# Float16 halves of the cached keys and values: made tile by tile in the attention units and kept in DRAM, instead of in the last stage

## Chip, cores and metric

One core of one Trainium2 chip. The metric is the device time of one launch in microseconds, the median of several runs; lower is better. A profiled execution is one more run, with the hardware profiler on.

## The reference, cut to what matters

One layer of a streaming encoder, for 2048 new frames of one prompt and for 16 new frames of each of 8 running streams that bring a cache of 512 positions. Two attention branches run beside each other on the same normalised input:

```python
# d = 1024; branch a: 4 heads of (2 x 64 keys, 128 values); branch b: 8 heads of 64
h = rms_norm(x) * (1 + scale) + shift
qa, ka, va, za, qb, kb, vb, zb, ga, gb = split(h @ w_in)         # qa, ka rotated by position
# a: two softmaxes over the keys, o = (p1 - lam * p2) @ va, mask by chunks of 64
# b: stick-breaking: a = sigmoid(z) * exp(sum of log_sigmoid(-z) over later keys), o = a @ vb, causal
ya = (rms_norm(oa) * 0.8 * silu(za)) @ w_branch_a
yb = (ob * silu(zb)) @ w_branch_b
y  = rms_norm(x + gate * ((sigmoid(ga) * ya + sigmoid(gb) * yb) @ w_out))
# the sample streams: the same, with keys = concat(cache_a_k, ka), values = concat(cache_a_v, va), and so for b
```

All inputs and outputs are float32. The four caches (`cache_a_k`, `cache_a_v`, `cache_b_k`, `cache_b_v`) are 8 x 512 positions x 512 numbers each, 8.4 MB. The outputs are the two results and the new keys and values.

## The kernel before

**Halves.** TensorE works on float16. To keep the accuracy of float32, an operand x is scaled by a power of two s and split into `hi` = float16(s x) and `lo` = float16(s x - hi), and a product takes three matmuls, hi*hi, hi*lo and lo*hi. `split` (line 294) makes the halves: `hi` on ACT, POOL or DVE, `lo` always on DVE with one `scalar_tensor_tensor`. The scale comes from a bound, the sum of squares of the whole operand: `sum_squares` (line 274) squares on ACT and adds along a row, `total` (line 215) adds over the 128 partitions with a matmul against a matrix of ones, and `scales` (line 221) cuts the exponent out of it with a few DVE steps on 1 to 16 columns, which gives s and 1/s.

**Stages.** A first stage computes the modulation and hT, the halves of the transposed normalised input, which stay in DRAM (`hT_d`). Then come eight *units* u = 0..7, one head of branch a (even u) or two heads of branch b (odd u) each. In a unit, tile t = NT is the sample's 128 rows and t = 0..15 are the prompt's. Three streams of work are interleaved on the engines: the projections (L435, with gates in L511), about five tiles ahead of the rest (`LEAD`), which load hT tile by tile into one of three `hs` buffers (`fetch_h`, L412); the scores of tile t (L646, L647), with the softmax (L565, L610) or the stick-breaking product (L623 scans on DVE, L629 on POOL); and the product of weights and values two tiles later (`PV_LAG`; L703 to L708), for which the weights' halves are transposed by a transfer within SBUF (`turn`, L587, into `wt`). Three PSUM banks "s" serve the scores. While unit u runs, `prepare_unit(u + 1)` loads and splits the next unit's weights into buffers of 4 KB per partition out of the list `free`; its pieces stand in `back`, a few of them per tile from the unit's first tile on.

**Squares of the caches.** The scale of a cached head needs the sum of squares of all of it. `norms` (line 845) makes a list `spare` of 80 pieces, each a load of 128 x 1024 numbers into a buffer of `free` and one square on ACT: 16 pieces of the branch and output weights and 64 of the caches (4 caches x 4 heads x 4 pieces). A tile with an empty `back` takes some of `spare` (lines 1264 to 1269), so they go where no unit is being prepared. The caches are loaded here for the squares alone and dropped.

**Last stage.** After the units, 17 tiles pass through the branch and output products (`branches` L1322, `turned`, `turned_y` L1172, `output` L1351); for each tile, `inputs` loads o, z and g from DRAM (L1180 to L1185), ACT makes sigmoids and halves. Beside the first 13 of them (`S_TILES`) runs the attention of the samples over the caches, `sample` (line 729), in a lane of steps, six of them later for each unit (`S_PERIOD`). Here each cached piece is loaded once more as float32 into one of three `dc` buffers (L755, L757). Keys are split with `hi` on ACT into `k16c` and then transposed within SBUF into `dks` (L764); values are split into `v16c` and used as they are. Scores of the samples are L782, outputs L810.

**Queues.** All transfers named here are issued by SP, in program order; an instruction that waits holds back what stands behind it. The order on every engine is made by the framework's scheduler from the order of the calls.

Of the kernel before, what the change touches and what calls it, by code (L numbers as in the profile page):

```python
# [16 lines left out]
F32 = mybir.dt.float32  # L17
# [32 lines left out]
S_PERIOD = 6  # L50
H_AT = 2
# [61 lines left out]
def layer_kernel(ctx: ExitStack, tc: tile.TileContext, a: dict):  # L113
# [6 lines left out]
    def act(**kw):  # L120
# [20 lines left out]
    values_by_block = {  # L141
        "av": a["cache_a_v"][0].rearrange("b (j p) h e -> p j b (h e)", p=P),
        "bv": a["cache_b_v"][0].rearrange("b (j p) h d -> p j b (h d)", p=P),
    }
# [29 lines left out]
    gate_d = dram.tile([9, D], F32, name="gate_d")  # L174

# [39 lines left out]
    def total(col, n=1):  # L215

        p = bank("t")
        T.matmul(p[:, 0:n], ones, col, start=True, stop=True)
        return p[:, 0:n]
# [62 lines left out]
    def add_up(acc, n):  # L282
# [4 lines left out]
        return col  # L287

    def add_up_all(acc):
        col = tiny.tile([P, acc.shape[1]], F32, tag="cols", name="cols", bufs=1)  # L290
        V.tensor_reduce(out=col, in_=acc, axis=AX.X, op=ALU.add)
        return col
# [107 lines left out]
    csums = con.tile([P, 16, 4], F32, name="csums")  # L400
# [328 lines left out]
    def sample(U, dec, qpad, cs, parity):  # L729
# [6 lines left out]
        sk, ik, sv, iv = (cs[:, i : i + 1] for n in (nk, nv) for i in (cache_column(n, h), 16 + cache_column(n, h)))  # L736
# [15 lines left out]
        def cache(name, i):  # L752
            box[name, i] = kc = dec.tile([P, 8, P], F32, tag="dc", name="dc", bufs=3)
            if name == nv:
                load(out=kc, in_=values_by_block[name][:, i, :, h * P : (h + 1) * P])  # L755
            else:
                load(out=kc, in_=caches[name][:, i * 8 : i * 8 + 8, h * P : (h + 1) * P])  # L757

        def keys(i):
            kc = box.pop((nk, i))  # L760
            k16 = dec.tile([P, 16, 2, 64], F16, tag="k16c", name="k16c", bufs=2)
            split(k16[:, :, 0, :], k16[:, :, 1, :], kc.rearrange("p j (c d) -> p (j c) d", c=2), sk, S)
            box["k", i] = kt = dec.tile([P, 8, 2, P], F16, tag="dks", name="dks", bufs=4)
            nc.sync.dma_start_transpose(out=kt.rearrange("p j c n -> p (j c) n"), in_=k16.rearrange("p j f d -> p (j f d)"))  # L764
# [671 lines left out]
```

## Time and profile before

| | |
|---|---|
| median of 3 runs | 2340.79 us (2339.63 to 2344.61) |
| the profiled execution | 2345.66 us |
| its span, first to last instruction | 2343.9 us |
| busy share of the span: PE, DVE, ACT, POOL | 90%, 73%, 71%, 28% |
| mean granted TensorE clock | 0.965 |
| moved by DMA | 445.29 MB in 834,498 packets, mean 190 GB/s |
| HBM read, written | 245.60 MB, 69.24 MB |

In the profile PE is TensorE (its weight loads apart as PEld), DVE VectorE, ACT ScalarE, POOL GpSimd and SP the engine that issues transfers. `L302` is line 302 of the kernel before. A row of a group has the instruction, what it writes and reads, its shape and count, and times; "idle before" and waits say how long an engine stood and what ended the wait. Matmuls overlap in the pipeline, so the mean time of one is longer than its share of PE.

### The profile page before, as it was taken

How to read it: one execution, taken by the hardware profiler on the slowest of the kernel's cores; microseconds unless marked ns; L12 is line 12 of the kernel's file. 1: busy time of each engine (PE TensorE's matmuls, PEld its weight loads, DVE VectorE, ACT ScalarE, POOL GpSimd, SP SyncE). 2: the span in 40 equal slices, each digit the busy share in tenths (PEclk: the TensorE clock that was granted, in tenths of full speed). 3: DMA queues.
4: the chain of work that ended last, by engine and by line, in shares of the span. 5: the costliest groups of instructions: out<-in, count | busy, mean ns of one | idle time of the engine just before them, and what ended most of it. 6: DMA issues, size and time to landing. Idle time of an engine off the chain costs nothing. (4 is left out here: it accounts for less than half of the span.)

```text
span 2343.9 us, 41533 instructions
## 1 busy us (share of the span) xinstructions
PE 2104.1 (90%) x14688; PEld 1119.9 (48%) x14688; DVE 1714.2 (73%) x3661; ACT 1656.7 (71%) x3260; POOL 664.1 (28%) x578
## 2 busy tenths in 40 slices
PE   5998898988989899899999989999996869788998
PEld 3654454545545445445545544554553434334443
DVE  4658765779865677978667797877778868777663
ACT  4968777788877788778677777866777656665641
POOL 1222022356400334630034473103345121111111
PEclk7999999999999999999999999999997989999999
DMA  9777659797785997877587877756687999998421
GB/s 335 274 213 177 154 117 275 175 201 166 208 204 126 219 203 190 174 184 188 134 194 174 189 171 180 195 145 145 148 177 167 284 253 242 240 241 239 147 102 48
DMA packets 834498, 445.29 MB, mean 190 GB/s; under 512 B 537354, under 2 KB 777274, under 8 KB 833776
## 3 DMA queue, kind: packets, MB, share of 16 engines
q1 hardware_dynamic: 833340, 442.24, 75.7%
q8 instruction: 115, 1.88, 0.3%
q14 instruction: 95, 0.78, 0.1%
q10 hardware_dynamic: 948, 0.39, 0.1%
HBM read 245.60 MB, written 69.24 MB: 134 GB/s over the span
## 5 line engine op out<-in xcount | busy, mean ns | idle before, releaser
L629 POOL TENSOR_TENSOR sc_p<-sc_p,sc_n 128x127 f32<-128x127 f32 (+7 forms) x192 | 313.4, 1637 | 826.7 <-DVE sc_n L623 813.0
L435 PE MATMUL ps_mm<-wb,hs 128*128 128x512 f16 x1632 | 415.9, 383 | 0.1
L435 PEld LDWEIGHTS <-hs 128*128 128x128 f16 x3120 | 274.8, 99 | 256.6 <-DMA hs<-hT_d 10.9
L435 PE MATMUL ps_mm<-wa,hs 128*128 128x512 f16 x1488 | 374.5, 382 | 10.6 <-DVE qbuf L470 6.7
L623 DVE TENSOR_TENSOR_SCAN sc_n<-ps_s,sc_n,zero_t 128x512 f32<-128x512 f32 x192 | 245.4, 1278 | 68.2 <-ACT ps_s L122 64.7
L646 PE MATMUL ps_s<-k,qst 128*128 128x512 f16 (+3 forms) x640 | 225.3, 353 | 32.7 <-DVE sc_n L623 24.1
L580 DVE TENSOR_TENSOR sc_n<-sc_p,sc_n 128x128 f16<-128x128 f32 (+7 forms) x192 | 212.6, 1111 | 57.1 <-ACT sc_n L579 56.7
L511 PEld LDWEIGHTS <-hs 128*128 128x128 f16 x1632 | 156.5, 98 | 188.0 <-ACT qst L539 6.1
L122 ACT ACTIVATE sc_p<-ps_s,usc 128x512 f32<-128x512 f32 (+3 forms) x320 | 204.7, 640 | 32.7 <-PE ps_s L647 25.2
L647 PE MATMUL ps_s<-k,qst 128*128 128x512 f16 (+3 forms) x640 | 225.9, 354 | 0.0
L579 ACT CAST sc_n<-sc_p 128x128 f16<-128x128 f32 (+7 forms) x192 | 155.4, 813 | 77.5 <-POOL sc_p L629 77.2
L707 PE MATMUL ps_o<-v,wt 128*128 128x128 f16 x1088 | 172.7, 226 | 36.9 <-DMA wt<-sc_n 36.8
L511 PE MATMUL ps_t<-wa,hs 128*128 128x512 f16 x816 | 193.2, 383 | 7.6 <-ACT qst L539 6.0
L122 ACT ACTIVATE ps_s<-ps_s,usc 128x512 f32<-128x512 f32 (+3 forms) x328 | 199.8, 609 | 0.0
L511 PE MATMUL ps_t<-wb,hs 128*128 128x512 f16 x816 | 191.5, 379 | 1.1 <-DVE fsq L343 0.6
L1351 PE MATMUL ps_o<-wo,wb 128*128 128x512 f16 x816 | 186.1, 382 | 5.6 <-ACT wb L1173 5.6
L708 PE MATMUL ps_o<-v,wt 128*128 128x64 f16 x1088 | 159.1, 199 | 0.0
L707 PEld LDWEIGHTS <-wt 128*128 128x128 f16 x1088 | 105.8, 102 | 104.5 <-DMA wt<-sc_n 50.5
L565 DVE TENSOR_SCALAR_CACHE_REDUCE sc_p<-ps_s,usc 128x512 f32<-128x512 f32 (+3 forms) x160 | 106.3, 665 | 44.5 <-PE ps_s L647 30.7
L623 DVE TENSOR_TENSOR_SCAN sc_n<-ps_s,zero_t 128x128 f32<-128x128 f32 (+3 forms) x128 | 104.1, 814 | 43.3 <-ACT ps_s L122 42.7
L565 DVE TENSOR_SCALAR_CACHE_REDUCE sc_n<-ps_s,usc 128x512 f32<-128x512 f32 (+3 forms) x160 | 106.3, 665 | 35.4 <-PE ps_s L647 25.5
L708 PEld LDWEIGHTS <-wt 128*128 128x128 f16 x1088 | 103.9, 101 | 55.0 <-issue 2.9
(357 smaller groups left out, 4440.5 us busy)
## 6 DMA issues: line engine op xcount, KB each, us to landing
hs<-hT_d SPq DMA_DIRECT2D x130, 512.0 KB, 4.2
g_d<-gt SPq DMA_DIRECT2D x68, 256.0 KB, 3.3
wb<-g_d SPq DMA_DIRECT2D x26, 512.0 KB, 6.3
out_dram<-pr SPq DMA_DIRECT2D x204, 64.0 KB, 1.9
o_d<-o SPq DMA_DIRECT2D x136, 64.0 KB, 2.5
hs<-o_d SPq DMA_DIRECT2D x17, 512.0 KB, 4.8
out_dram<-x SPq DMA_DIRECT2D x17, 512.0 KB, 2.7
wide<-in_w_ada_dram SPq DMA_DIRECT2D x8, 1024.0 KB
```

What stands on the lines that cost most here:

```text
L122: i = S.activation(**kw)
L435: T.matmul(box["p"], box["h"][:, hi, k, :], U["w"][k][:, wi, :], start=(n == 0), stop=(n == 3 * KT - 1))
L511: T.matmul(box["g"][:, 0:gw], box["h"][:, hi, k, :], U["wg"][k // per][:, k % per, wi, :], start=(j == 0), stop=(j == 3 * KT - 1))
L565: V.tensor_scalar(out=dst[:, lo : lo + n], in0=p[:, 0:n], scalar1=sc_pos, scalar2=None, op0=ALU.mult, op1=ALU.max, accum_out=job["mx"][:, ...
L580: V.tensor_tensor(out=lo, in0=src, in1=hi, op=ALU.subtract)
L623: V.tensor_tensor_scan(out=dst[:, lo : lo + n][:, ::-1], data0=src[:, 0:n][:, ::-1], data1=zero_t[:, 0:1].to_broadcast([P, n]), initial=fi ...
L629: G.tensor_tensor(out=p[:, 0:m], in0=p[:, 0:m], in1=n[:, 1 : m + 1], op=ALU.mult)
L646: T.matmul(p[:, 0:n], qst[:, c, :], kk[:, c, 0:n], start=True, stop=False)
L647: T.matmul(p[:, 0:n], qst[:, 2 + c, :], kk[:, c, 0:n], start=False, stop=not diag)
L707: T.matmul(po[:, c * P : (c + 1) * P], wt[:, wj, :], vt[:, c, :, :], start=first, stop=False)
L708: T.matmul(po[:, c * P : c * P + 64], wt[:, nb + wj, :], vt[:, c, 0, :], start=False, stop=last)
L1351: T.matmul(po, st["y"][:, yi * 8 + k, :], wo[j * 4 + k // 2][:, wi, k % 2, :], start=(n == 0), stop=(n == 3 * KT - 1))
```

## The change

The squares of the caches no longer serve one scale per head. Each piece of 128 x 1024 numbers gets a scale of its own, as soon as its own square is there, and its halves are made at once, in the units, and written to DRAM in two new families of tensors, `keys_d` and `values_d`. `spare` thus holds for the caches 66 stages instead of 64 pieces; stage k halves piece k - 2, squares piece k - 1 and loads piece k, so that each step of a piece is a tile apart. Halving a piece takes the sum over partitions (a matmul into a bank "s"), four DVE steps on one column, `hi` on POOL, `lo` on DVE and a write of 512 KB. Values are loaded with two transfers instead of one, into the order in which the last stage wants them.

`spare` is now dealt out by tile, with `spare_at`: from tile 7 on in unit 0, in all prompt tiles of units 2, 4, 6, and in tiles 0 to 7 of units 1, 3, 5; a tile may have work of `back` and of `spare`.

In the last stage nothing is split any more. Keys come by a transposing transfer straight from `keys_d` into `dks` (now six buffers), values by a load of 4 KB per partition from `values_d` into `v16c` (now four). A unit's lane has 10 steps (`S_LONG`) instead of 13. The scales' inverses are made from the exponents kept in `cexp`; they differ by piece, which is by pair of streams, so `cs` gets them by groups of 32 partitions.

```diff
+S_LONG = 10
...
+    keys_d = {(n, h, i): dram.tile([P, 16, P], F16, name=f"keys_{n}{h}{i}") for n in ("ak", "bk") for h in range(4) for i in range(4)}
+    values_d = {(n, h): dram.tile([P, 4, NB, 2, P], F16, name=f"values_{n}{h}") for n in ("av", "bv") for h in range(4)}
...
-    def total(col, n=1):
+    def total(col, n=1, tag="t"):
-        p = bank("t")
+        p = bank(tag)
...
-        def cache(name, i):
-            box[name, i] = kc = dec.tile([P, 8, P], F32, tag="dc", name="dc", bufs=3)
-            if name == nv:
-                load(out=kc, in_=values_by_block[name][:, i, :, h * P : (h + 1) * P])
-            else:
-                load(out=kc, in_=caches[name][:, i * 8 : i * 8 + 8, h * P : (h + 1) * P])
-
         def keys(i):
-            kc = box.pop((nk, i))
-            k16 = dec.tile([P, 16, 2, 64], F16, tag="k16c", name="k16c", bufs=2)
-            split(k16[:, :, 0, :], k16[:, :, 1, :], kc.rearrange("p j (c d) -> p (j c) d", c=2), sk, S)
-            box["k", i] = kt = dec.tile([P, 8, 2, P], F16, tag="dks", name="dks", bufs=4)
-            nc.sync.dma_start_transpose(out=kt.rearrange("p j c n -> p (j c) n"), in_=k16.rearrange("p j f d -> p (j f d)"))
+            box["k", i] = kt = dec.tile([P, 8, 2, P], F16, tag="dks", name="dks", bufs=6)
+            nc.sync.dma_start_transpose(out=kt.rearrange("p j c n -> p (j c) n"), in_=keys_d[nk, h, i].rearrange("p j n -> p (j n)"))
+
+        def values(j):
+            box["v", j] = v16 = dec.tile([P, NB, 2, P], F16, tag="v16c", name="v16c", bufs=4)
+            load(out=v16, in_=values_d[nv, h][:, j, :, :, :])
...
-        def values(i):
-            vc = box.pop((nv, i))
-            box["v", i] = v16 = dec.tile([P, 8, 2, P], F16, tag="v16c", name="v16c", bufs=2)
-            split(v16[:, :, 0, :], v16[:, :, 1, :], vc, sv, S)
...
+        steps = [[] for _ in range(S_LONG)]
+        steps[0] += [one(fetch)]
         for i in range(4):
+            steps[i // 2] += [one(keys, i)]
+            steps[4 + i // 2] += [one(values, i)]
+            steps[7 + i // 2] += [one(output_cached, i)]
+        steps[2] += [one(queries)]
+        steps[4] += [one(scores_all)]
+        steps[9] += [one(finish)]
...
+        def fetch(name, h, i):
+            st = free.pop(0)
+            src = caches[name][:, i * 8 : i * 8 + 8, h * P : (h + 1) * P]
+            if name in ("av", "bv"):
+                for b in range(2):
+                    load(out=st.rearrange("p (j b n) -> p j b n", j=4, b=2)[:, :, b, :], in_=src[:, 4 * b : 4 * b + 4, :])
+            else:
+                load(out=st.rearrange("p (j n) -> p j n", n=P), in_=src)
+            fetched.append((st, name, h, i))
+
+        def square():
+            acc = tiny.tile([P, 1], F32, tag="cacc", name="cacc", bufs=2)
+            sum_squares(fetched[0][0], 1024, acc)
+            squared.append((*fetched.pop(0), acc))
+
+        def halve():
+            st, name, h, i, acc = squared.pop(0)
+            c = tiny.tile([P, 3], I32, tag="csc", name="csc", bufs=2)
+            f = cexp[:, cache_column(name, h), i : i + 1]
+            V.tensor_scalar(out=c[:, 0:1].bitcast(F32), in0=total(acc, 1, "s"), scalar1=2.0 ** -46, scalar2=None, op0=ALU.max)
+            V.tensor_scalar(out=f, in0=c[:, 0:1], scalar1=24, scalar2=None, op0=ALU.logical_shift_right)
+            V.tensor_scalar(out=c[:, 1:2], in0=f, scalar1=-1.0, scalar2=204.0, op0=ALU.mult, op1=ALU.add)
+            V.tensor_scalar(out=c[:, 2:3], in0=c[:, 1:2], scalar1=23, scalar2=None, op0=ALU.logical_shift_left)
+            to = free.pop(0)
+            w = P if name in ("av", "bv") else P // 2
+            x = to.bitcast(F16).rearrange("p (j f n) -> p j f n", f=2, n=w)
+            split(x[:, :, 0, :], x[:, :, 1, :], st.rearrange("p (j n) -> p j n", n=w), c[:, 2:3].bitcast(F32), G)
+            if name in ("av", "bv"):
+                load(out=values_d[name, h][:, :, 2 * i : 2 * i + 2, :, :], in_=x.rearrange("p (j b) f n -> p j b f n", b=2))
+            else:
+                load(out=keys_d[name, h, i], in_=x.rearrange("p (j c) f d -> p j (c f d)", c=1))
+            free.append(st)
+            free.append(to)
...
+        def stages(k):
+            if k > 1:
+                halve()
+            if 0 < k <= len(todo):
+                square()
+            if k < len(todo):
+                fetch(*todo[k])
...
+    def spare_at(u, t):
+        return u < 7 and t < NT and (t >= 7 if u == 0 else u % 2 == 0 or t < 8)
...
-            if back:
-                for fn in back[: -(-len(back) // max(1, (W_READY if u else W_READY + 2) - t % NT))]:
-                    back.pop(0)()
-            elif n > 3:
-                for _ in spare[: -(-len(spare) // ((NT + 1 - t % NT) + 8 * (6 - min(u, 6))))]:
+            for fn in back[: -(-len(back) // max(1, (W_READY if u else W_READY + 2) - t % NT))]:
+                back.pop(0)()
+            if spare and spare_at(u, t):
+                left = sum(spare_at(*step) for step in steps[n:])
+                for _ in spare[: -(-len(spare) // left)]:
                     spare.pop(0)()
...
-        cs = scales(total(add_up_all(csums), 16), res, "s_c", 16)
+        inv = res.tile([P, 16, 4], I32, name="inv")
+        V.tensor_scalar(out=inv, in0=cexp, scalar1=50.0, scalar2=None, op0=ALU.add)
+        V.tensor_scalar(out=inv, in0=inv, scalar1=23, scalar2=None, op0=ALU.logical_shift_left)
+        cs = res.tile([P, 16], F32, name="cs")
+        for i in range(4):
+            V.tensor_copy(out=cs[i * 32 : i * 32 + 32, :], in_=inv.bitcast(F32)[i * 32 : i * 32 + 32, :, i])
```

More of the change, by code (lines that the diff above doesn't have):

```diff
@@ L286, in add_up @@
         V.tensor_reduce(out=col, in_=acc[:, 0:n], axis=AX.X, op=ALU.add)
[L287 to L291, printed above, removed]
         return col
```

29 lines of the change are left out of this document (6 added, 23 removed).

## The prediction

> **What bounds the kernel now.** I read the page first, then the busy times by stage, then the DMA answer, the waits and the tiles of the stage that the change empties, and last the rows that price what it adds. First the page's head:
>
> ```profile
> span 2343.9 us, 41533 instructions
> ## 1 busy us (share of the span) xinstructions
> PE 2104.1 (90%) x14688; PEld 1119.9 (48%) x14688; DVE 1714.2 (73%) x3661; ACT 1656.7 (71%) x3260; POOL 664.1 (28%) x578
> ```
>
> PE is the main engine, but 90% is a mean over stages. L629 runs on POOL in the stick-breaking units alone, so POOL's busy time shows where units begin and end, and I cut the stages there. The first three rows are units 2, 4 and 6 (even: differential attention), the fourth is the part of the last stage that works on the cached keys and values, the next three the first thirds of units 1, 3 and 5, the last two late tiles of units 1 and 3. The columns are the stretch, its length, busy us of each engine, the granted clock, the share of time in which the DMA engines were busy, and GB/s.
>
> ```profile
> core 0: us, PE busy (x) PEld busy (x) DVE busy (x) ACT busy (x) POOL busy (x), PEclk, DMA share, GB/s
> 580.00:755.00 175.00, 165.24 (x1157) 91.94 (x1156) 121.48 (x327) 133.04 (x299) 28.20 (x32) 0.98 0.74 180
> 1010.00:1170.00 160.00, 155.06 (x1105) 85.81 (x1103) 118.20 (x314) 119.25 (x271) 24.68 (x29) 1.00 0.69 172
> 1430.00:1590.00 160.00, 156.26 (x1119) 87.11 (x1118) 125.03 (x331) 120.03 (x268) 28.51 (x32) 1.00 0.71 177
> 1816.00:2168.00 352.00, 288.19 (x2102) 137.40 (x2101) 267.47 (x546) 218.87 (x282) 61.79 (x41) 0.94 0.98 250
> 340.00:420.00 80.00, 72.57 (x459) 36.74 (x457) 51.92 (x100) 63.67 (x135) 27.29 (x22) 0.96 0.96 240
> 755.00:835.00 80.00, 70.59 (x445) 36.01 (x444) 51.07 (x93) 61.19 (x131) 25.71 (x22) 0.98 0.90 223
> 1170.00:1250.00 80.00, 73.22 (x461) 36.93 (x460) 50.57 (x97) 59.61 (x128) 27.89 (x23) 0.98 0.77 192
> 527.40:586.00 58.60, 52.08 (x440) 29.65 (x439) 55.50 (x114) 46.89 (x105) 35.84 (x32) 1.00 0.75 166
> 937.60:996.20 58.60, 49.13 (x424) 27.89 (x423) 58.19 (x91) 45.75 (x93) 40.56 (x34) 1.00 0.83 174
> ```
>
> So there are two regimes. In the even units PE sets the pace: 94%, 97% and 98% busy, with DVE at 69 to 78% and DMA at 69 to 74%. In the 352 us from 1816 PE is busy for 82% and the DMA engines for 98%: this stretch is bound by DMA, and the granted clock falls to 0.94 there. Its DMA answer and its longest waits:
>
> ```profile
> DMA packets 156727, 87.88 MB, mean 250 GB/s; under 512 B 81967, under 2 KB 143158, under 8 KB 156699
> ...
> dc<-in_cache_a_v_dram SPq DMA_DIRECT2D x16, 512.0 KB, 6.1
> dc<-in_cache_b_k_dram SPq DMA_DIRECT2D x16, 512.0 KB, 5.6
> dc<-in_cache_b_v_dram SPq DMA_DIRECT2D x15, 512.0 KB
> dc<-in_cache_a_k_dram SPq DMA_DIRECT2D x13, 512.0 KB, 6.6
> ...
> dks<-k16c SPq DMA_TRANSPOSE x32, 7.3
> ```
> ```profile
> ACT k16c L297 <- DMA dc<-in_cache_b_k_dram: 29.1, 13, 4.8
> DVE k16c L302 <- ACT k16c L297: 28.3, 13, 6.2
> ACT wb L122 <- DMA wb<-g_d: 24.4, 10, 4.9
> ACT k16c L297 <- DMA dc<-in_cache_a_k_dram: 24.2, 12, 7.3
> ```
> ```profile
> PE ps_s L782 <- DMA dks<-k16c: 9.3, 5, 3.7
> ```
>
> The columns of a wait are total us, times and the longest. ACT stands 53 us before the keys' halves for a transfer, DVE 28 us behind ACT; both serve their queues in order, so the tile work behind (u16, y16, the sigmoids) comes late, and PE with it. PE itself names the keys' transposes for 9.3 us only.
>
> **What goes from the last stage.** The loads of `dc` and these four groups (min/median/max ns):
>
> ```profile
> L297 ACT ACTIVATE k16c<-dc,s_c x32: 1142/1148/1158, 1816.8 to 2159.5; 128x1024 f16<-128x1024 f32 x32
> L302 DVE SCALAR_TENSOR_TENSOR k16c<-dc,s_c,k16c x32: 1269/1283/2315, 1818.0 to 2160.7; 128x1024 f16<-128x1024 f32 x32
> L297 ACT ACTIVATE v16c<-dc,s_c x32: 1132/1144/1160, 1846.7 to 2204.3; 128x1024 f16<-128x1024 f32 x32
> L302 DVE SCALAR_TENSOR_TENSOR v16c<-dc,s_c,v16c x32: 1271/1283/2332, 1848.6 to 2206.3; 128x1024 f16<-128x1024 f32 x32
> ```
>
> That is 64 x 1.15 = 73 us of ACT and 64 x 1.28 = 82 us of DVE; neither is the bound there, so by themselves they are worth nothing. What counts is DMA. In the window 29 key loads vanish (0.524 MB each, 15.2 MB); 31 value loads keep their bytes but come in 128 runs of 4 KB instead of 1024 of 512 B; the 32 transposes stay, with DRAM as source. If the engines' time goes by bytes, the stretch needs 352 x (87.9 - 15.2)/87.9 = 291 us of DMA; if by packets, 352 x (156,727 - 29 x 1024 - 31 x 896)/156,727 = 223 us. Either way PE is late next: its 288.19 us at the 96% of the even units (mean of the three rows) are 300 us. I take 300, **52 us gained**. At the 90% of the odd units' first thirds it is 320 (32 gained); the best is DMA by bytes, 291 (61 gained), which PE can follow since at full clock its work is 288.19 x 0.94 = 271 us. SP gains too: its transposes of keys wait for no half any more, only for one of six `dks` buffers. The new sums for `cs` (six DVE steps in place of seven and a PE step) are nothing, and the tail after the samples stays as it is.
>
> The transposes' source is what no row shows: the nearest are these same transposes out of SBUF (7.3 us to landing) and the 512-byte reads of DRAM (5.6 to 6.6 us). I take the SBUF price, since size and packets are the same; twice that price is a rival below. The Trainium skill ("DMA: Bandwidth & Descriptors", section "Why small descriptors are slow (HBM only)") speaks against the change: transfers within SBUF escape the small-piece penalty, while 256-byte pieces of HBM lose 27%. By it, an estimate, 32 transposes of 2.1 us would take 18 us more DMA, 309 instead of 291, and the gain would be some 43. No run so far shows it.
>
> **What the units get.** Loads and squares of the pieces were there (64 of each) and stay; `spare_at` deals them one to a tile over all of units 2, 4, 6 and the first eight tiles of 1, 3, 5 (82 items on 81 tiles; the first 16 are weights, so unit 1 gets hardly any halves). Counting from there, units 2, 4 and 6 each halve 16 pieces, 3 and 5 eight each. Per piece:
>
> ```profile
> L299 POOL TENSOR_SCALAR wo<-x,s_w x4: 1118/1194/1919, 1809.8 to 1837.6; 128x1024 f16<-128x1024 f32 x4
> ```
> ```profile
> L228 DVE TENSOR_SCALAR sc_f<-sc_q x41: 135/154/171, 41.2 to 2256.8; 128x1 int32<-128x1 int32 x23, 128x2 int32<-128x2 int32 x17, 128x16 int32<-128x16 int32 x1
> ```
> ```profile
> 592.20 0.28 PE L218 MATMUL ps_t<-col,ones 128*128 128x1 f32 x2
> 592.34 0.38 PE L435 MATMUL ps_mm<-wb,hs 128*128 128x512 f16 x1
> ```
> ```profile
> out_dram<-x SPq DMA_DIRECT2D x17, 512.0 KB, 2.7
> ```
> ```profile
> SPq L587 <- DVE sc_n L580: 80.5, 55, 4.0
> ```
>
> PE: a sum over partitions holds the next matmul back by 0.14 us (592.20 to 592.34), 64 x 0.14 = 9 us, all of it on the path where PE is the bound. POOL: 1.19 us, 76 in all, hidden (28 of 160 us busy in an even unit). DVE: 1.28 + 4 x 0.154 = 1.9 us, 30 us per even unit, which takes unit 4 from 118 to 149 of 160 us (93%). DMA: a write of 512 KB, at most 2.1 us at the 250 GB/s of the saturated stretch, less by packets (128 of 4 KB); its upper end is the 2.7 us in which such a write landed. Of unit 4's own DMA answer (1010 to 1170 us) these rows say that it issued 8 of the 16 loads that it will have:
>
> ```profile
> DMA packets 57786, 27.51 MB, mean 172 GB/s; under 512 B 36184, under 2 KB 55371, under 8 KB 57771
> ...
> wb<-in_cache_b_k_dram SPq DMA_DIRECT2D x8, 512.0 KB
> ```
>
> By bytes it goes from 0.69 x 160 = 110 us to 110 + 8 x 2.1 + 16 x 2.1 = 160 of 160; by packets (8 x 1024 for the loads and 16 x 320 for the writes, keys 128 and values 512 runs each, onto 57,786) to about 135. SP: each write waits in its queue for DVE's half, behind it stand the `wt` transposes and the hT loads; the nearest row, transposes that wait for DVE's half, has 80.5/55 = 1.5 us a time, 94 us over all 64, covered by two tiles of `PV_LAG` and three `hs` buffers as long as it stays near that. A PSUM bank of "s" is lent to each sum.
>
> So in the even units DVE and DMA come close to PE. How much of PE's 96% is lost is the open price. Rows with DMA at 0.77 to 0.96 and the preparation of a unit beside it (340, 755 and 1170) have PE at (72.57 + 70.59 + 73.22)/240 = 90%; those with DVE at 95% and 99% have 89% and 84%. Lower end: nothing but PE's own 2.2 us a unit; upper end: 84%. I take 92%, nearer to the first group, because the late half of an even unit has no preparation beside it: (165.24 + 2.2)/0.92 = 182, (155.06 + 2.2)/0.92 = 171, (156.26 + 2.2)/0.92 = 172 us, together 525 for 495, **30 us lost**. Units 3 and 5 have their loads in the first third now as then; the halves cost PE 1.1 us each and some waiting: 3 us each, **6 us lost**. Unit 1 gives its load burst back, which I count at nothing.
>
> Sum: 2345.66 us (the profiled execution; 4.9 above the median) - 52 + 36 = 2329.7, so against the median **2325 us**.
>
> **Rivals.** (a) *The units hide more*: at 95% the even units lose 14 us, the odd ones 4; with PE at unit 6's 98% in the last stage (288.19/0.98 = 294, 58 gained) that is 2301. For it: unit 2, with almost its full number of loads today, still has 94%. (b) *DVE becomes the bound of the even units* (the slower side). DVE's half reads two SBUF tensors while POOL reads SBUF for the next piece; the maxima 2315 and 1919 above are about one operation plus the other (1.28 + 1.12 = 2.40), so one can wait for the other's whole. 16 x 1.1 us more puts unit 4's DVE at 167 of 160 us. PE then falls to the 86% of the two late rows: 195 + 183 + 184 = 562 for 495, 67 lost, 8 in the odd ones, less 52: 2364. It decides from where PE in the even units is under 89.5%. The Trainium skill ("SBUF — State Buffer", section "SBUF: two separate sides") has this as a rule: the two engines share a pair of ports under an exclusive lock, and the loser blocks fully. By that rule, the trace's maxima agree. Against it: POOL is idle for four fifths of an even unit. (c) *Transposes out of DRAM cost the engines twice*: 16.8 MB more in bytes, 89.5 MB, 358 us, so the last stage gains nothing and the units still pay 36: 2377. It takes the gain to the units' price at 1.7 times. (d) *Both sides are equal*: 2341.
>
> That the halves would not leave the last stage can be excluded: in the built program's order no split of `dc` is left there.
>
> **Numbers.** Forecast 0.42; (a) 0.11; (d) 0.09; (b) 0.27; (c) 0.11. Faster by over 0.2% (4.7 us, about what a measurement of this kernel can tell from no change) 0.53, within 0.09, slower 0.38. The likeliest case alone reaches from 2308 to 2336. The range 2296 to 2368 leaves out the better part of (a), most of (c) and the top of (b).
>
> **What would show it.** Right: in the sample stretch PE at 95% or more, DMA under 0.95, ACT waiting for no key; even units of 182, 171 and 172 us with DVE over 90%; the sums at 0.14 us of PE. Wrong: a sample stretch of 330 us or more, transposes that land later than 7.3 us while DMA stays at 0.98 (c), or even units over 190 us with PE waiting for DVE (b).

## The result, and the profile after

The changed kernel takes **2364.27 us** (median of 4 runs, 2357.52 to 2368.53), the kernel before 2341.86 in the same comparison: ratio **1.0096, 95% interval 1.0075 to 1.0116**, slower. The forecast was 2325. The profiled execution is the fastest of the four (2357.52 us) and that of before lies 4 above its median, so the traces hold 12 of the 22 us.

```profile
span 2355.7 us, 42219 instructions
## 1 busy us (share of the span) xinstructions
PE 2110.6 (90%) x14814; PEld 1136.7 (48%) x14814; DVE 1747.4 (74%) x3917; ACT 1591.2 (68%) x3196; POOL 742.6 (32%) x642
```

As in the prediction the page's shares say little, and the stages say more. From here on a unit ends with its last product of weights and values on PE, and "the units" are units 1 to 7 together. Before (columns as in the prediction): all of these units, then units 2, 4, 6, then the samples' stretch of the last stage.

```profile
327.20:1807.10 1479.90, 1368.95 (x9653) 739.13 (x9652) 1131.77 (x2245) 1134.95 (x2392) 520.99 (x438) 0.98 0.77 180
565.10:750.40 185.30, 175.41 (x1224) 97.25 (x1221) 135.96 (x359) 139.62 (x318) 34.18 (x39) 0.98 0.74 182
991.30:1168.90 177.60, 171.80 (x1217) 94.66 (x1214) 133.80 (x359) 133.34 (x306) 32.28 (x39) 1.00 0.68 169
1408.40:1585.80 177.40, 171.46 (x1223) 95.14 (x1220) 137.08 (x366) 133.31 (x304) 35.43 (x40) 1.00 0.70 172
1807.20:2223.00 415.80, 346.98 (x2516) 165.70 (x2514) 313.11 (x655) 255.39 (x334) 73.60 (x50) 0.94 0.91 238
```

After, the same five:

```profile
329.40:1882.00 1552.60, 1399.28 (x9781) 759.99 (x9779) 1246.47 (x2561) 1137.10 (x2391) 605.65 (x502) 0.97 0.79 191
564.30:766.50 202.20, 186.46 (x1275) 103.41 (x1273) 162.18 (x436) 139.67 (x318) 53.66 (x54) 0.97 0.84 224
1014.20:1218.40 204.20, 183.72 (x1262) 102.12 (x1260) 156.36 (x432) 138.99 (x315) 51.40 (x51) 0.97 0.83 217
1460.60:1659.90 199.30, 179.31 (x1234) 99.03 (x1233) 158.36 (x431) 138.94 (x311) 50.78 (x52) 0.97 0.81 209
1882.00:2243.00 361.00, 332.36 (x2548) 164.86 (x2547) 232.75 (x599) 190.62 (x275) 68.18 (x51) 0.98 0.82 228
```

The last stage, samples and tail, goes from 536.8 to 473.7 us, **63 gained**; the units from 1480 to 1553, **73 lost**, 65 of them in units 2, 4, 6 (540 to 606 us; single units compare only roughly, since the scheduler also moves projections between them: 39 matmuls, some 8 us, came from the odd units into these three). 55 of the 63 lie in the samples' stretch, 8 in the tail. Over all, PE has exactly the 128 records more that the 64 sums bring (9653 to 9781). Its time in the units can be split into three: what it stands idle (length less busy), 111 us before and 153 after; what half-speed clock costs, next paragraph, 32 and 49; and the rest, its work, 1337 and 1350. So the 73 us are **42 of waiting, 17 of clock and 13 of sums**.

**The clock.** The trace's clock record comes in windows of 3.41 us, each at full or at half speed: 19 half windows in the units before, 29 after, 1.7 us lost in each. They follow idleness: PE was idle for 65% and 69% of the window just before a half one on average, for 5% and 6% before a full one, and no full window follows one that was idle for more than 58%. Four consecutive windows of unit 4 after, and PE's wait there:

```profile
1104.00:1107.40 3.40, 3.40 (x21) 1.71 (x20) 2.56 (x6) 3.40 (x10) 1.12 (x1) 1.00 0.97 258
1107.40:1110.80 3.40, 0.82 (x4) 0.20 (x2) 3.37 (x12) 1.62 (x7) 0.00 (x0) 0.98 1.06 177
1110.80:1114.20 3.40, 3.06 (x24) 2.51 (x25) 0.64 (x2) 1.10 (x1) 0.00 (x0) 0.51 0.39 114
1114.20:1117.70 3.50, 3.19 (x35) 2.23 (x33) 3.35 (x11) 2.29 (x8) 0.00 (x0) 1.00 0.49 160
```
```profile
PE ps_o L697 <- DMA wt<-sc_n: 2.9, 1, 2.9
```

PE waits 2.9 us for one `wt`, and the following window runs at 0.51: the wait costs 4.6 us. The Trainium skill ("TensorE: Matmul & The Clock Gate", section "HAM oscillation — how this bites in real kernels") warns of idle gaps over about 3.4 us; here shorter ones were enough.

**The waits.** PE's longest in the units, before and after (total us, times, longest):

```profile
PE ps_o L707 <- DMA wt<-sc_n: 36.8, 29, 4.8
PE ps_s L646 <- DVE sc_n L623: 24.1, 34, 2.5
PE ps_o L703 <- DMA wt<-sc_n: 16.2, 11, 3.9
...
PE ps_mm L435 <- DMA hs<-hT_d: 3.0, 2, 1.6
```
```profile
PE ps_o L701 <- DMA wt<-sc_n: 37.8, 24, 6.0
PE ps_s L640 <- DVE sc_n L617: 34.7, 36, 5.0
PE ps_o L697 <- DMA wt<-sc_n: 29.6, 15, 3.6
PE ps_mm L429 <- DMA hs<-hT_d: 14.5, 14, 2.7
```

Three grow: for score banks that DVE empties (+11; behind the scans, so in the odd units), for the even units' `wt` (+13), for hT (+12, 8 of them in the even units). None is long; there are more of them. Ahead of the 2.9 us above, SP was at this (start, length, transfer):

```profile
1098.02 1.85 SPq L323 DMA_DIRECT2D wb<-in_w_in_dram  x2
1099.98 0.86 SPq L486 DMA_DIRECT2D out_dram<-pr  x1
1100.88 0.49 SPq L489 DMA_DIRECT2D z_d<-pr  x1
1101.41 0.51 SPq L323 DMA_DIRECT2D wb<-in_w_in_dram  x1
1101.97 0.70 SPq L424 DMA_DIRECT2D rope<-in_shapes_dram  x1
1102.76 0.93 SPq L841 DMA_DIRECT2D wa<-in_cache_a_v_dram  x2
1103.79 1.44 SPq L424 DMA_DIRECT2D rope<-in_shapes_dram  x1
1105.32 0.38 SPq L485 DMA_DIRECT2D out_dram<-rot  x1
1105.93 0.33 SPq L691 DMA_DIRECT2D o_d<-o  x1
1106.35 4.18 SPq L581 DMA_TRANSPOSE wt<-sc_n  x2
```

DVE had the tile's low halves ready at 1102.6, with this:

```profile
1102.22 0.35 DVE L296 SCALAR_TENSOR_TENSOR sc_n<-sc_p,r,sc_n 128x128 f16<-128x128 f32 x1
```

SP came to the first of their two transposes at 1106.35, behind the loads and stores that stand before it in its order, and the two held it until 1110.5, while the DMA engines were fully busy (1.06 in that window).

**The chain.** To compare kernels, each tile's maximum on DVE (L587) in units 2, 4, 6 is paired with the issue of its last `wt` transpose, in the order of the tiles. From one to the other lie ScalarE's exponentials, DVE's sums, both halves and SP's queue. It takes 12.6 us on average before and 15.3 after (48 tiles, which scatter from 6 to 30 us). PE has a part in it too: meanwhile DVE and ACT also stand still for matmuls, 1.4 and 1.2 us a tile before, 0.7 and 1.2 after; so that is not what grew. The expectations below quote 10.4, 10.3 and 12.1 us instead: averages over the 37 to 44 tiles of a kernel that a first pairing took in.

### The profile page after: what moved, and what is told of

It reads as the page before. It is cut to its first block, busy times and chain, and to the rows that moved or that the text cites. A ratio compares the mean times of both kernels' runs of the same rounds, so it can differ in the third digit from the quotient of the medians.

```text
span 2355.7 us, 42219 instructions
## 1 busy us (share of the span) xinstructions
PE 2110.6 (90%) x14814; PEld 1136.7 (48%) x14814; DVE 1747.4 (74%) x3917; ACT 1591.2 (68%) x3196; POOL 742.6 (32%) x642
## 5 line engine op out<-in xcount | busy, mean ns | idle before, releaser
L429 PE MATMUL ps_mm<-wb,hs 128*128 128x512 f16 x1734 | 447.4, 384 | 7.4 <-DMA hs<-hT_d 6.0
L429 PE MATMUL ps_mm<-wa,hs 128*128 128x512 f16 x1386 | 358.8, 385 | 10.8 <-DMA hs<-hT_d 8.5
L505 PE MATMUL ps_t<-wb,hs 128*128 128x512 f16 x816 | 205.0, 383 | 3.5 <-DVE qst L533 2.3
L505 PE MATMUL ps_t<-wa,hs 128*128 128x512 f16 x816 | 198.2, 383 | 6.4 <-ACT qst L533 6.4
L701 PE MATMUL ps_o<-v,wt 128*128 128x128 f16 x1088 | 168.7, 226 | 37.8 <-DMA wt<-sc_n 37.8
L697 PE MATMUL ps_o<-v,wt 128*128 128x128 f16 x544 | 103.7, 225 | 31.0 <-DMA wt<-sc_n 31.0
L1381 PEld LDWEIGHTS <-wb 128*128 128x128 f16 x816 | 78.8, 98 | 96.1 <-issue 2.7
```

Source lines behind the costliest of these rows:

```text
L429: T.matmul(box["p"], box["h"][:, hi, k, :], U["w"][k][:, wi, :], start=(n == 0), stop=(n == 3 * KT - 1))
L505: T.matmul(box["g"][:, 0:gw], box["h"][:, hi, k, :], U["wg"][k // per][:, k % per, wi, :], start=(j == 0), stop=(j == 3 * KT - 1))
L701: T.matmul(po[:, c * P : (c + 1) * P], wt[:, wj, :], vt[:, c, :, :], start=first, stop=False)
L1381: T.matmul(po, st["y"][:, yi * 8 + k, :], wo[j * 4 + k // 2][:, wi, k % 2, :], start=(n == 0), stop=(n == 3 * KT - 1))
```

## The experiments

Times are medians, beside that of the kernel before in the same comparison. The other columns come from the one profiled execution of each kernel, which was up to 3 us off the median, but 5 above it for the kernel before and 6 to 11 below it for the changed kernel, before_dealt, values_only and writes_pool. Idle and clock are PE's in the units, as above; all in us. In no_writes, no_halves, neither, neither_held, lo_pool and pool_alone something that the result needs is left out; the other versions do the whole computation.

| kernel | time | before | units | idle | clock | last stage | chain |
|---|---|---|---|---|---|---|---|
| before (profile) | | 2340.8 | 1480 | 111 | 32 | 537 | 12.6 |
| changed | 2364.3 | 2341.9 | 1553 | 153 | 49 | 474 | 15.3 |
| writes_pool | 2379.0 | 2346.6 | 1556 | 152 | 55 | 480 | 14.5 |
| no_writes | 2366.1 | 2346.6 | 1550 | 153 | 50 | 480 | 14.0 |
| no_halves | 2351.6 | 2346.6 | 1536 | 143 | 54 | 484 | 14.8 |
| lo_pool | 2354.8 | 2346.6 | 1543 | 149 | 49 | 481 | 13.5 |
| before_dealt | 2349.6 | 2345.9 | 1477 | 107 | 37 | 539 | 12.2 |
| alone | 2387.8 | 2345.9 | 1578 | 172 | 58 | 481 | 14.4 |
| fixed | 2364.6 | 2345.9 | 1552 | 160 | 56 | 482 | 13.7 |
| neither | 2311.8 | 2345.9 | 1502 | 114 | 43 | 481 | 13.4 |
| gap | 2356.9 | 2348.7 | 1536 | 148 | 34 | 486 | 14.2 |
| late | 2374.7 | 2348.7 | 1563 | 162 | 43 | 483 | 14.5 |
| pool_alone | 2341.1 | 2347.4 | 1530 | 138 | 46 | 482 | 12.5 |
| low_pool2 | 2393.5 | 2347.4 | 1580 | 180 | 50 | 478 | 13.6 |
| keys_only | 2351.4 | 2347.4 | 1515 | 134 | 36 | 505 | 13.0 |
| values_only | 2363.9 | 2347.4 | 1528 | 145 | 42 | 499 | 13.7 |
| neither_held | 2314.6 | 2350.3 | 1500 | 117 | 39 | 482 | 13.1 |
| hi_act | 2388.7 | 2350.3 | 1571 | 165 | 61 | 486 | 15.7 |
| keys_gap | 2355.4 | 2350.3 | 1516 | 138 | 32 | 508 | 13.4 |

The theories began with one cause each: SP's queue (1), VectorE (2), DMA's bytes (3), the work's place (4), the sums and, in another round, the buffers (both called 5). When these had failed, the chain (6) and two separate waits (7) took their place.

**writes_pool** (SP's queue)

```diff
-                load(out=keys_d[name, h, i], ...)
+                G.dma_start(out=keys_d[name, h, i], ...)      # and so for values_d
```


> The 64 writes of halves are issued from POOL's queue instead of SP's; bytes, halves and buffers stay. The changed kernel takes 2364 us, its seven units 74 us more than before's. Theory 1 (a write that waits for its half stands on SP's queue ahead of the transposes of the weights and of the loads of hT, and PE waits for these): the even units lose the waits for wt and hs, some 30 to 40 of their 56 us, and the time is 2325 to 2335. Theory 2 (VectorE: the low half and the four small instructions stand ahead of the softmax chain): within 5 us of 2364. Theory 3 (the 32 MB written slow the other transfers): within 5 us of 2364, as the bytes are the same.

2378.97 (ratio 1.0139, 1.0097 to 1.0180), slower still. The even units' `wt` waits only fall from 29.6 to 25.1 us, those for hT from 14.5 to 2.8, before's value, and all idle time ahead of the scores grows from 44 to 60. Theory 1's forecast fails: taking the writes off SP does not bring the time back. But the edit isn't pure: a write that POOL issues goes by another, software queue, and POOL is busy for 38 us more in the units (644 us), so what SP alone costs isn't shown by it.

```profile
PE ps_o L697 <- DMA wt<-sc_n: 25.1, 20, 4.7
...
PE ps_mm L429 <- DMA hs<-hT_d: 2.8, 3, 1.8
```
```profile
q0 software_dynamic: 9216, 33.56, 3.9%
```

**no_writes** (bytes)

```diff
+            if h > 0:
+                pass
+            elif name in ("av", "bv"):
```


> All halves are made, but only those of head 0 of each cache are written, and the last stage reads head 0's for all heads: three quarters of the writes are left out, with what the last stage reads the same in size. Theory 1 (SP's queue): three quarters of the waits go, 2335 to 2345, like the kernel with the writes on POOL's queue. Theory 3 (bytes): 2325 to 2335, and more than the kernel with the writes on POOL's queue gains. Theory 2 (VectorE): within 5 us of 2364.

2366.10 (1.0080, 1.0055 to 1.0106): theories 1 and 3 miss by 21 and 31 us. Yet one wait answers: the even units' `wt` are back near before's 16.2, while the score banks' waits, which split over more releasers, stay, and so do those for hT.

```profile
PE ps_s L640 <- DVE sc_n L617: 26.8, 37, 2.4
PE ps_o L697 <- DMA wt<-sc_n: 18.4, 12, 3.8
PE ps_mm L429 <- DMA hs<-hT_d: 13.4, 12, 3.7
PE ps_s L640 <- DVE sc_p L559: 8.8, 6, 2.8
```

**no_halves** (the other half of the work)

```diff
+            if h > 0:
+                load(out=raw_k[name, h, i], in_=st)          # raw_v for values
+                free.append(to); free.append(st)
+                return
```


> All pieces are written, but for heads 1 to 3 of each cache the float32 piece itself is written, to DRAM that nothing reads; the high and the low half of these are left out (the sums and scales are made), and the last stage reads head 0's halves for all heads. The bytes are those of the changed kernel; 48 of 64 halves of POOL and of DVE are gone, and a write waits for nothing that is not long done. Theory 1 (SP's queue): 2335 to 2345, as the writes no longer hold the queue. Theory 2 (VectorE): 2325 to 2340, with the softmax chains of the even units as short as before's. Theory 3 (bytes): within 8 us of 2364.

2351.61 (1.0026, 1.0011 to 1.0042), between the theories. Here it is the other way about: the score banks wait as before, the `wt` do not.

```profile
PE ps_o L699 <- DMA wt<-sc_n: 32.4, 14, 8.5
PE ps_s L642 <- DVE sc_n L619: 23.8, 36, 2.4
```

From the low half's end to the issue of its transpose it takes 2.7 us here, 1.1 before; from the maximum to the weighting of the softmax, 5.8 and 5.7. In no_writes these are 1.0 and 6.8. So writes lengthen the chain at SP's queue, halves on DVE, by 1 to 2 us each.

**lo_pool** (VectorE's own half)

```diff
-            split(x[:, :, 0, :], x[:, :, 1, :], ..., G)
+            for f in range(2):
+                G.tensor_scalar(out=x[:, :, f, :], in0=s3, scalar1=s, scalar2=0.0, op0=ALU.mult, op1=ALU.add)
```


> The low half is made on POOL as a second copy of the high one, so that VectorE makes none; the subtraction is left out. Bytes and queues stay; the write waits for POOL's two instructions of 1.2 us each instead of one on POOL and one on DVE. Theory 2 (VectorE's work of 64 times 1.3 us, or the port that POOL and VectorE share): 2325 to 2345 if it is VectorE's own work; little or nothing if it is the shared port, which POOL now takes twice as long. Theory 1 (SP's queue): 2360 to 2370, as the write waits no less. Theory 3 (bytes): within 5 us of 2364.

2354.80 (1.0044, 1.0026 to 1.0062): of 22 us, 14 go with DVE's half, although POOL makes a second copy in its place; fewer than theory 2 had.

**before_dealt** and **alone** (the place): after's dealing in the kernel before, and before's in the changed one.

```diff
-                for _ in spare[: -(-len(spare) // left)]:                     # alone
+            if not busy and n > 3:
+                for _ in spare[: -(-len(spare) // ((NT + 1 - t % NT) + 8 * (6 - min(u, 6))))]:
```


> The kernel before with one edit: its loads and sums of cached pieces are dealt to the tiles by the changed kernel's rule (beside the work of preparing the next unit, more of it in the even units), not by its own (only in tiles where nothing is prepared). No halves, no writes, no sums on TensorE. Theory 4 (the place of the work costs the units, not its kind): its units take 40 to 60 us more than the 1480 of before, and the time is 2380 to 2400. The other theories (the halves, the sums on TensorE with the small instructions behind them, the buffers, the writes): within 8 us of before's 2342.

> The changed kernel with the rule of before for where its load, sum and halve steps go: only in tiles in which nothing of the next unit is prepared. Theory 4 (the place): the units lose 40 to 60 of the 74 us added, 2305 to 2325. The other theories: the same work in fewer tiles, two to three steps in a tile, 2360 to 2375.

2349.64 (1.0023, 1.0006 to 1.0041) and 2387.81 (1.0188, 1.0167 to 1.0209). Dealt after's way, before's units are no longer than they were (1477 us), and crowding the changed kernel's steps costs more, beyond every forecast: theory 4 falls.

**fixed** (the sums)

```diff
-            V.tensor_scalar(out=c[:, 0:1].bitcast(F32), in0=total(acc, 1, "s"), ...)
+            V.tensor_scalar(out=c[:, 0:1].bitcast(F32), in0=acc, ...)
```


> Each row's scale is made from the row's own sum of squares: the sum over the rows on TensorE is left out, so a piece's scales no longer wait for TensorE nor does TensorE wait for a bank or for ScalarE's sum. Theory 5 (the sums: 66 matmuls of 0.14 us that stand in TensorE's queue behind ScalarE, and VectorE's first small instruction that stands for them, 28.6 us in all by the waits): 2325 to 2340. Theory 4 (the place): 2355 to 2362, the 9 us of the matmuls at most. Theory 2 (VectorE's halves): 2350 to 2362.

2364.56 (1.0085, 1.0065 to 1.0104). PE's work in the units falls to 1336 us, before's value, so the sums do cost some 13 (the kernels with all 64 sums lie between 1339 and 1358); idle and clock take as much back. Theory 5 falls, and no forecast holds.

**neither** (halves and writes)

```diff
+            if h > 0:
+                free.append(st)
+                return
```


> For heads 1 to 3 of each cache neither halves nor writes: the pieces are loaded, summed and scaled, and the last stage reads head 0's halves for all heads; three quarters of the new work of POOL, VectorE and DMA are left out. If the price of the halves (2364 to 2352 without three quarters of them) and that of the writes (none measured) add up: 2345 to 2355, and what is left of the units' price is that of place or sums. If writes and halves each hide the other (whichever stays is enough): 2310 to 2330, units within 20 us of before's 1480.

2311.80 (0.9856, 0.9833 to 0.9880), at the edge of the second forecast: units 1502. Halves and writes hide each other. Each against before in its own comparison, the changed kernel is 22 us slower; without three quarters of the writes 20 slower, without three quarters of the halves 5 slower, without both 34 faster. So halves and writes together are the better part of the price: without three quarters of them 51 of the 73 us are gone.

**gap** and **late** (place within the tile), and **before_dose**

```diff
+        run(in_gap)          # softmax_pair, behind the exponentials: sum, four steps, high half (gap alone)
...
+        run(behind)          # behind turn(): low half and write; late: both behind the tile
```


> The changed kernel with its halve step taken apart and moved, nothing left out: in the even units the sum, the small instructions and POOL's high half stand behind the four exponentials' issue, where VectorE waits for ScalarE anyway, and VectorE's low half and the write on SP's queue stand behind the tile's own wt transposes; the load of the next piece comes ahead of both and takes a buffer whose write is a tile old. In the odd units all of it stands behind the tile. Theory 6 (what costs is the softmax chain: from the maximum to the issue of the wt transpose 10.4 us in before, 10.3 without halves and writes, 12.1 in the changed kernel, and the even units' time follows it; halves lengthen it on VectorE, writes and loads on SP's queue, and each alone by as much as both): the chain is back under 11 us, the units take 1500 to 1515 and the time is 2305 to 2325. If the even units' price comes from the work itself (bytes, ports, POOL), wherever it stands: 2355 to 2370.

> The same taking apart, but the whole halve step stands behind the tile's other work in even units too, which on VectorE and SP is where it stood, one tile on; only the load's place ahead of it, and with that its buffer, are other. Theory 6: VectorE's part still stands ahead of the next tile's maximum, 2350 to 2370. Theory 5 (a load on SP's queue waits for the write of the tile before from the same buffer, 14 us in an even unit): 2335 to 2345.

> The kernel before with two VectorE sums over 1024 columns of a constant, some 2 us together, ahead of each tile of units 2, 4 and 6, where the changed kernel's VectorE makes its halves; nothing waits for them but what follows on VectorE. Theory 6: VectorE's instructions ahead of the chain delay it whoever's they are, units 25 to 50 us longer, 2365 to 2390. If VectorE, at 75% in these units, has the room and the price needs POOL, the waits for TensorE or the buffers: within 8 us of before's 2345.

gap 2356.88 (1.0036, 1.0020 to 1.0052), late 2374.66 (1.0111, 1.0081 to 1.0141). gap takes 17 us off the units, most of it clock (34 us instead of 49), and shortens the chain by only 1.1 us; its time is the one forecast for a price that comes from the work itself, and theory 6's forecast fails. late lies above both its forecasts: the load's other buffer gains nothing. before_dose, 2412.11 (1.0275, 1.0247 to 1.0304), says nothing: its sums depend on no data of the tile, and the scheduler put them all at the start of the program, where the first stage grew by 58 us, while the units stayed at 1486:

```profile
L1273 DVE TENSOR_REDUCE dose<-ones x96: 1161/1207/1220, 1.2 to 146.4; 128x8 f32<-128x1024 f32 x96
```

That is also a warning for the rest: every kernel here gets an order of its own on every engine, PE included.

**pool_alone** (a quarter of the writes, no half on DVE)

> The kernel without three quarters of the writes (the last stage reads head 0's halves) and, beside that, with the low half made on POOL as a second copy of the high one, so that VectorE makes no half; the subtraction is left out. Theory 7 (two separate waits of TensorE: 18 us more for score banks that VectorE empties, where it makes low halves, and 12 to 14 us more for the wt transposes of the even units, where pieces are written, each with a half-clock window now and then behind it): both are gone, 2318 to 2335, units 1505 to 1520. If POOL's work counts (its port, or POOL as an engine), 2345 to 2360.

2341.09 (0.9978, 0.9964 to 0.9992), between the two. The `wt` wait is back (14.5 us), the idle time ahead of the score matmuls partly (36 us; 44 in the changed kernel, 26 before). With 29 us more than neither, POOL's copies have a price of their own (there are two to a piece here, one in the changed kernel), so theory 7 is not all.

**low_pool2** (all of it on POOL)

```diff
+            G.tensor_scalar(out=s3, in0=s3, scalar1=s, scalar2=0.0, op0=ALU.mult, op1=ALU.add)
+            G.tensor_tensor(out=x[:, :, 1, :], in0=s3, in1=x[:, :, 0, :], op=ALU.subtract)
```


> Nothing is left out: the low half is made on POOL in full, as a scaling of the piece in place and a subtraction, so that VectorE makes no half and POOL has three instructions a piece instead of one. Theory 7: TensorE's idle time ahead of the score matmuls falls from 44 us to about 30, that ahead of the even units' weighted sums stays at about 30; 2345 to 2357, near the 2355 of the kernel with a second copy. If POOL's time (some 5 to 6 us a piece, half of an even tile) comes into a chain (the stick weights of the odd units, the write): 2360 to 2375.

2393.51 (1.0201, 1.0168 to 1.0233): slower than either forecast. The score matmuls' idle time falls to 38 us, not 30, and the even units' `wt` waits grow to 46.0.

**keys_only** and **values_only**: the other cache summed in the units and split in the last stage, as before.

> Only the keys' halves are made in the units and kept in DRAM; the values are summed in the units and loaded in float32 and split in the last stage as before, in the same number of steps. Nothing is left out. If price and gain both go by the piece: units 1516, last stage 505, 2350. If the price is more than linear in the work of a tile (as halves and writes hide each other): units 1500 to 1510. If the last stage's gain comes from the keys (their 512-byte rows, ScalarE's split, the transposes): last stage 480 to 490, 2315 to 2335; if from the values: 520 to 530, 2360 to 2370.

> The other way about: the values' halves are made in the units, the keys are summed there, and loaded, split and transposed from the buffer in the last stage as before, which keeps before's thirteen steps for a sample unit. Nothing is left out. If price and gain go by the piece, 2350; if the last stage's gain comes from the keys, its length stays at 520 to 535 and the time is 2360 to 2375; if from the values, 480 to 495 and 2315 to 2335.

2351.41 (1.0015, 1.0000 to 1.0031) and 2363.89 (1.0066, 1.0043 to 1.0089). Keys alone cost the units 35 of 73 us and bring the last stage 32 of 63, values 48 and 38: price and gain go roughly by the piece, though values cost more than they bring: by the medians keys alone are 4 us slower than before, values alone 17.

**neither_held**, **hi_act**, **keys_gap**

```diff
+            to = free.pop(0)                      # neither_held, h > 0: taken and given back
...
-            split(..., G)
+            split(..., S)                         # hi_act
```


> The kernel without halves and writes for heads 1 to 3, but its pieces take a second buffer from the list and give both back, as the changed kernel does; nothing is written to it. The work is that of the kernel at 2312 us; only the order in which buffers come round differs. If the 28 us between that kernel and the one with POOL's two copies are the buffers' (a load on SP's queue reuses a buffer that came back one step earlier): 2330 to 2345. If they are POOL's work: 2305 to 2320.

> Nothing is left out: the high half is made on ScalarE (1.07 us a piece by the sums' row) instead of POOL. If POOL's work costs by itself (VectorE's instructions that overlap it are some 0.1 us longer each, 19 us in all in units 2 to 6, and the low half stands for it): 2335 to 2355. If ScalarE's exponentials then stand behind the halves and the chain from the maximum to the transpose grows past 12 us: 2370 to 2390.

> Keys alone halved (2351 us: units 35 over before's 1480, last stage 32 under its 537) with the halve step taken apart and put behind the exponentials and behind the wt transposes (which took 16 us of 72 off the units where all 64 pieces are halved, and gave 12 back in the last stage of that run). If these go by the piece: units 1507, last stage 505 to 511, 2340 to 2348, no different from before. If the rest of the chain gains more at the smaller load: 2325 to 2338, faster than both kernels.

2314.62 (0.9843), 2388.72 (1.0159) and 2355.40 (1.0018, 1.0006 to 1.0030). The buffers' round costs nothing; ScalarE is a worse place for the high half than POOL, as forecast and with the longest chain, 15.7 us; and the gap's edit brings nothing at half the load, where both forecasts were lower. No version that keeps the whole computation beats the kernel before.

**What holds of it.** Shown is what the price consists of (waits of PE, half-speed clock, sums) and what it comes from: halves and writes together, and not the place among the tiles, the order of the buffers or the bytes alone. How they bring it about isn't shown. Over these 18 kernels (before_dose apart) and before itself, the length of units 2, 4, 6 goes with the chain at a correlation of 0.76, some 22 us for each us of chain over 48 tiles. That fits an account in which what is put ahead of a tile's softmax on DVE, ScalarE or SP brings its `wt` later, PE waits, and the clock follows. But it is a correlation, and there is evidence against it as the whole cause. low_pool2 has the longest even units (636 us) at a chain of 13.6, and pool_alone has 575 at before's chain, where before has 540. And over neither, halves alone (no_writes) lengthen the chain by 0.5 us, writes alone (no_halves) by 1.3, both by 1.9, so the chain adds up, as far as 48 scattered tiles can tell; the length of units 2, 4 and 6 does not: 50, 56 and 51 us. Why halves and writes don't add up in time stays open, since the order on the engines can't be held fixed from one kernel to the next.

## Why the prediction was wrong

- **The last stage** came out as forecast, in part by luck: 52 forecast, 63 measured, and 51 to 63 in the kernels with all halves in DRAM. DMA is no longer full: its share in the samples' stretch fell to 0.82, 296 us of 361 (291 were forecast by bytes for a shorter cut of it), and ACT waits for no key any more. But PE's share is 92%, not 96%. The prediction's rule gives 346.98/0.96 = 361 us for this stretch, just what was measured, because two errors cancel: PE's busy time fell to 332 us as the clock rose from 0.94 to 0.98, and the share came out lower. And the tail, which was to stay as it is, gave 8 us. ACT's longest wait there, and from the DMA answer of the same stretch:

```profile
ACT wb L123 <- DMA wb<-g_d: 52.2, 16, 7.2
```
```profile
DMA packets 106304, 82.31 MB, mean 228 GB/s; under 512 B 84635, under 2 KB 85787, under 8 KB 106274
...
dks<-keys_ak SPq DMA_TRANSPOSE x16, 7.4
```

- **Transposes out of DRAM** were priced rightly at SBUF's: 7.4 us to landing, 7.3 before (medians of the few whose landing the traces tell, 3 and 4 of 32). Rival (c) is out, since the stage gained. The Trainium skill's rule ("DMA: Bandwidth & Descriptors", section "Why small descriptors are slow (HBM only)") would, by the prediction's estimate, have left a gain of 43; the runs gave more.
- **The units** were the step that failed: 36 us forecast, 73 measured. The sum had 9 us of the sums on PE and 27 of waiting; measured were 13, 42, and 17 of half-speed clock, for which it had no term. Most of that lies in units 2, 4 and 6. The PE share of 92% taken for them means, for whole units, (518.7 + 6.6)/0.92 = 571 us for 540: 7 us of sums and 24 of waiting. They took 606: 35 more of waiting, 14 more of clock (3 to 17 us) and 17 more of work (8 for the 40 sums that fall into them, 8 for projections that came from odd units). By busy time their share was 90.7% (549.5 of 605.7 us), which looks close to 92%. But busy time includes half-speed time, and so the share hid it: the clock went from 0.98 to 1.00 down to 0.97, although the rows that the 92% was taken from already showed 0.96 to 0.98. A sum held PE for 0.2 us, not 0.14, which was one row.
- **Rival (b)** has the right time, 2364, and part of its sign came, PE waiting longer for DVE (41 us ahead of score matmuls, 26 before). Its mechanism didn't: DVE isn't the bound of the even units, with 162.18 of 202.20 us in unit 2 (80%), 77% and 79% in 4 and 6; these waits are mostly in the odd units; and without DVE's half 2355 was still measured. What it said of the port that POOL and DVE share is seen, small: DVE's instructions that overlap a half on POOL in units 2 to 6 are 13 to 20 us longer in all than others of their form, depending on which others are taken. That agrees with the Trainium skill ("SBUF — State Buffer", section "SBUF: two separate sides") in kind.
- **Writes on SP** "covered by two tiles of `PV_LAG` and three `hs` buffers": not covered. SP's waits at the writes are as small as assumed (46 us for 48 pieces in the even units), but PE waits 13 us more for `wt` where there are writes (29.6 against 16.2) and not where three quarters of them are gone (18.4). A write landed in 3.8 us (median of 13 known landings), above the 2.7 that the prediction took as the upper end.
- **POOL hidden**: wrong as well. Two copies of each piece on POOL, with a quarter of the writes and no half on DVE (pool_alone), take 29 us more than neither; what the one copy of the changed kernel costs isn't shown.
- **Rival (a)**, that the units hide more, would need the price that was left in neither (units 22 us over before's, 2312), where three quarters of halves and writes are gone. Its reason, that unit 2 had nearly all its loads and still 94%, says nothing of halves and writes.

## What to carry to other kernels

Where an engine is 96% busy with four in-order queues feeding it, the price of added work isn't found by asking whether another engine becomes full: at 80% DVE and 0.83 DMA, 64 small jobs cost 73 us. Split PE's time into idle, half-speed and work before taking a "share" from a row, and give each its own term in the sum. Look at the latency chain of one tile too, and ask for every added instruction whether it stands ahead of it; here it fits a part of the price, and isn't shown to set it. Removing one suspect alone can show little where a second one suffices by itself: remove both at once first.

## What the runs showed of the hardware

- A wait of 2 to 3 us on PE can cost 1.7 us more: windows of 3.41 us mostly go to half speed when PE was idle for half or more of the window before (17 of the 19 half windows in the units before, 27 of the 29 after, 437 of 536 over all 20 traces). No full window in the units of any trace follows one that was idle for more than 60%; 84 of 8443 follow one that was idle for half or more.
- A transposing transfer of 512 KB out of DRAM lands about as fast as one out of SBUF: 7.4 and 7.3 us after and before; over all traces 7.3 us in the median of 51 known landings out of DRAM (4.7 to 11.7), 6.9 of 14 out of SBUF (4.8 to 8.1).
- A sum over partitions on TensorE, one column against a matrix of ones in float32, takes 0.2 us of PE's time: in the changed kernel the next matmul starts 0.196 us after it in the median of 64.
